# First feed-forward of a two-block transformer: one product in plain float32 from unsplit weights, a new order of the four products, and the first norms reordered

## The chip, the cores and the metric

The kernel runs on one core of one Trainium2 chip. The metric is the device time of one execution in microseconds (us); lower is better. The kernel before took 975.63 us, the median of three runs (975.62, 975.63 and 975.93).

## The reference

The input `x` has 256 positions of 1024 values, and everything is float32. A first block of two layers is followed by a second block. Of the first layer, which is where the change lies, the reference computes:

```python
h = _multiscale_pool(x, pool_w, pool_scale)      # causal window means (2, 4, 8, 16) minus x, times four 256x256 matrices
x = _layernorm(ALPHA * x + h, ln_mix_g[0], ln_mix_b[0])
x = _layernorm(ALPHA * x + _swiglu(x, w_gate[0], w_up[0], w_down[0]), ln_ffn_g[0], ln_ffn_b[0])
```

`_swiglu` is `(silu(x @ w_gate) * (x @ w_up)) @ w_down` with a hidden width of 2816. After that come a differential attention layer with its own feed-forward, and a second block (three token mixers, a gated merge, a feed-forward with a squared relu and a final norm). All of that is untouched by the change.

## The kernel before, in words

**Tiles and products.** The 256 positions are two tiles of 128 rows, `xs[0]` and `xs[1]`. A product is made to float32 accuracy from three fast products: each operand is split into a high part (a rounded copy) and a low part (operand minus high part), and `mm3` (L315 to L317) issues high times high, high times low and low times high, all in the fast `float32r` type. `XTh` and `XTl` hold the two parts of the transposed activations. `x_transposed` makes them: four transposes on TensorE into a bank of PSUM (L393), a copy on ScalarE for the high part (L308), a subtraction on VectorE for the low part (L309).

**The weight stream.** The class `Stream` carries every weight matrix in *units* of 1 MB, each in two *halves* of 512 KB. `load` puts a half into one of `RAW_BUFS` = 5 raw buffers by DMAs on SyncE's queue (L61); `high` rounds it on ScalarE into `wh` (L92); `low` subtracts on VectorE into `wl` (L101), which frees the raw buffer, and then calls `load` again. Four units can be split ahead of their use (`W_BUFS`). `need(u)` forces what is still missing of unit u, `release` gives a unit's room back, and `side.tick()`, called after each group of products, runs the lows that are outstanding and up to two more highs. Each engine works through its instructions in the order in which they are written here, so a place in the source is a place in the engine's queue.

**The start.** The DMAs are written out by hand: `xs[0]`, the pool weights `pw`, `xs[1]`, a band matrix, then `st.load(2)`, the norm's bias `ln_mix_b`, then `st.load()`. In `load` the line `n = f // len(srcs)` gives a new value to the name that holds the bound, so that the call with 2 goes on until the raw buffers are full.

The pool layer is a small pipeline of its own: `pool_diff` (L704) makes the window differences of a tile on TensorE, `from_psum` (L712) copies them out on ScalarE, `add_tail` (L717) adds to tile 1 what windows take from tile 0, and `pool_product` (L722) multiplies by `pw` in plain float32. In the program a plain float32 matmul is one call, and in the trace it is two instructions. `ln` (L400 to L426) then works on one tile: scaling and residual on VectorE (L408, L409), the mean (L411, L412), the squares on ScalarE (L398), the centred value times gain (L419), the variance (L421), a power on GpSimd (L385), and the last line with the bias (L426). `ln` takes two callbacks, `first` after the squares and `then` after the power, in which the caller puts other work.

**The four products.** `swiglu` calls `ffn`. Its first two chunks of 256 hidden columns (`n_a` = 2) are computed row-wise, for each tile and chunk one bank of 128x512 (gate and up side by side). One product of tile and chunk uses two units (k-tiles 0 to 3 and 4 to 7 of the 1024 inputs): `proj_wide` (L330) issues 12 matmuls of 512 columns for each, 24 in all. Chunk 0 uses units 0 and 1 (halves 0 to 3), chunk 1 uses units 2 and 3 (halves 4 to 7). The order is tile 0 chunk 0, tile 0 chunk 1, tile 1 chunk 0, tile 1 chunk 1. In the middle of the second of them `next(pending)` transposes tile 1. After a product comes its nonlinearity (`post_a`, L596 and L597), and the result is transposed (L542) in the middle of what follows. From the third chunk on, `proj_b` works on both tiles at once with 256 columns.

Of the kernel before, what the change touches and what calls it, by code (L numbers as in the profile page):

```python
# [11 lines left out]
F32 = mybir.dt.float32  # L12
# [5 lines left out]
P = 128  # L18
D = 1024
T = 256  # L20
KT = D // P
D_FF = 2816
# [12 lines left out]
RAW_BUFS = 5  # L35
# [7 lines left out]
class Stream:  # L43


    def __init__(self, nc, pool, units, spare, spare_tile):
        self.nc, self.pool, self.units, self.spare, self.spare_tile = nc, pool, units, spare, spare_tile
        self.raw, self.w, self.pending, self.room = {}, {}, [], W_BUFS
        self.limit = 2 * len(units)
        self.n_dma = self.n_high = self.n_low = self.n_used = 0  # L50

    def load(self, n=None):

        n = 2 * len(self.units) if n is None else n
        while self.n_dma < min(n, self.n_low + RAW_BUFS):
            i = self.n_dma
            srcs, (n_k, f) = self.units[i // 2]
            self.raw[i] = self.pool.tile([P, n_k // 2, f], F32, tag="raw", name=f"raw{i}", bufs=RAW_BUFS)
            n = f // len(srcs)
            for j, src in enumerate(srcs):  # L60
                self.nc.sync.dma_start(self.raw[i][:, :, j * n:(j + 1) * n],  # L61
                                       src[:, i % 2 * (n_k // 2):(i % 2 + 1) * (n_k // 2)])
            self.n_dma += 1

    def high(self, force=False):
        i = self.n_high
        u, half = divmod(i, 2)
        if i >= self.n_dma or i >= self.limit and not force or not half and not self.room and u not in self.spare:
            return False
        n_k, f = self.units[u][1]  # L70
        if not half:
            self.w[u] = [], []
            if u in self.spare:
                self.tiles = [[self.spare_tile("bias", (n_k // 2, f)) for _ in range(2)],
                              [self.spare_tile("qk", (n_k // 4, f)) for _ in range(4)]]
# [12 lines left out]
        n = 0  # L88
        parts = []
        for h in hs:  # L90
            raw = self.raw[i][:, n:n + h.shape[1]]
            self.nc.scalar.copy(h, raw)  # L92
            parts.append((l[:, n:n + h.shape[1]], raw, h.bitcast(F32)))
            n += h.shape[1]
        self.pending.append(parts)
        self.n_high += 1
        return True
# [64 lines left out]
def model_kernel(ctx: ExitStack, tc: tile.TileContext, a: dict, out: bass.AP, stop=None):  # L162
# [13 lines left out]
    def bank(tag):  # L176
        return ps.tile([P, 512], F32, tag=tag, name=nm(tag), bufs=BANKS[tag])
# [4 lines left out]
    def small(n):  # L182
        return gen("sm", (n,))
# [25 lines left out]
    def bcast(src, n=D):  # L209
        t_ = gen("bc", (n,))  # L210
        load(t_, bass.AP(src.tensor, src.offset, [[0, P], [1, n]]))
        return t_
# [69 lines left out]
        load(pw[:, 4 * h:4 * h + 4], a["pool_w"][0, 2 * h:2 * h + 2].rearrange("g (k p) d -> p (g k) d", p=P))  # L282
    load(xs[1], x2[P:T])
    load(band[1], a["c_band"][:, :, 144:272])
    st.load(2)
    ln_gb = ln_g, bcast(a["ln_mix_b"][0])
    st.load()
    side = Side(st)

# [24 lines left out]
    def mm3(o, lh, ll, rh, rl, first, last):  # L314
        nc.tensor.matmul(o, lhsT=lh, rhs=rh, start=first, stop=False)  # L315
        nc.tensor.matmul(o, lhsT=lh, rhs=rl, start=False, stop=False)  # L316
        nc.tensor.matmul(o, lhsT=ll, rhs=rh, start=False, stop=last)  # L317
# [9 lines left out]
        if tick:  # L327
            side.tick()

    def proj_wide(o, t, u, h):  # L330

        wh, wl = st.need(u)
        s = slice(t * P, (t + 1) * P)
        for k in range(KT // 2):
            mm3(o, XTh[:, 4 * h + k, s], XTl[:, 4 * h + k, s], wh[k], wl[k], h == 0 and k == 0, h == 1 and k == 3)
        if t:
            st.release(u)
# [59 lines left out]
    def square(x, acc_col, bias=0.0):  # L397
        nc.scalar.activation(gen(shape=(x.shape[-1],)), x, AF.Square, bias=bias, scale=1.0 / 32.0, accum_out=acc_col)  # L398

    def ln(t, acc, g, b, scale=None, first=None, then=None):  # L400

        x = xs[t]
        sums, var, nm, nm32 = small(2), small(2), small(1), small(1)
        for h, c in enumerate(HALF):
            mix = acc[h]
            if scale is not None:
                mix = gen()
                nc.vector.tensor_mul(mix, acc[h], scale[:, c])  # L408
            nc.vector.scalar_tensor_tensor(x[:, c], x[:, c], ALPHA, mix, op0=ALU.mult, op1=ALU.add,  # L409
                                           accum_out=sums[:, h:h + 1])  # L410
        nc.vector.tensor_scalar(nm32, sums[:, 0:1], sums[:, 1:2], -1.0 / (32.0 * D), op0=ALU.add, op1=ALU.mult)  # L411
        nc.vector.tensor_scalar(nm, sums[:, 0:1], sums[:, 1:2], -1.0 / D, op0=ALU.add, op1=ALU.mult)  # L412
        for h, c in enumerate(HALF):
            square(x[:, c], var[:, h:h + 1], nm32)
        if first:
            first()
        y = [gen(), gen()]
        for h, c in enumerate(HALF):
            nc.vector.scalar_tensor_tensor(y[h], x[:, c], nm, g[:, c], op0=ALU.add, op1=ALU.mult)  # L419
        v = small(1)  # L420
        nc.vector.tensor_scalar(v, var[:, 0:1], var[:, 1:2], LN_EPS, op0=ALU.add, op1=ALU.add)  # L421
        rstd = rsqrt(v)
        if then:
            then()
        for h, c in enumerate(HALF):
            nc.vector.scalar_tensor_tensor(x[:, c], y[h], rstd, b[:, c], op0=ALU.mult, op1=ALU.add)  # L426

# [100 lines left out]
        side.tick()  # L528
        return e1

    def ffn(n_mats, nch, n_a, post_a, gate_b, post_b, end, pending, n_next=4, quota=0, n_late=3, aside={}):
        hT = {}
        us = [st.take(n_mats) for _ in range(n_a)]
        per_bank = 2 // n_mats
# [10 lines left out]
                split_from(tb[:, i * 256:(i + 1) * 256].rearrange("p (k c) -> p k c", k=2),  # L545
                           hT[c][0][:, :, s], hT[c][1][:, :, s])

        for t in range(2):
            for c0 in range(0, n_a, per_bank):
                b = bank("mm")  # L550
                mine = [us[c0 + i // n_mats][i % n_mats] for i in range(2)]
                for i, u in enumerate(mine):
                    proj_wide(b, t, u, i)
                    if not i and not t and c0 + per_bank == n_a:
                        next(pending, None)
                        st.limit = 2 * len(units)
                    if i:
                        if todo:
                            transposed(*todo.pop())
                        mid = post_a(b)  # L560
                    side.tick()
                todo.append((mid, range(c0, c0 + per_bank), t))
        acc = None
        late = []
        for c in range(n_a, nch):
# [24 lines left out]
            return acc, late[-1:], late  # L590
        return finish_layer(acc, end, late[-1:], late, n_next, quota)

    def swiglu(n_a, end, pending, n_next, quota, aside):
        def post_a(b):
            s, m = gen(shape=(256,)), gen(shape=(256,))
            nc.scalar.activation(s, b[:, 0:256], AF.Silu)  # L596
            nc.vector.tensor_mul(m, s, b[:, 256:512])  # L597
            return m

        def gate_b(b):  # L600
            s = gen()
            nc.scalar.activation(s, b, AF.Silu)  # L602
            return s

        def post_b(s, b):
            nc.vector.tensor_mul(s, s, b)
            return s

        return ffn(2, D_FF // 256, n_a, post_a, gate_b, post_b, end, pending, n_next, quota, aside=aside)

# [115 lines left out]
    d0 = [from_psum(pool_diff(0, i), 0, i) for i in range(3)]  # L726
    pb = [pool_product(d0, h) for h in range(2)]
    b1 = [pool_diff(1, i) for i in range(3)]
    d1 = [from_psum(b1[0], 1, 0)]
    st.high()  # L730

    def first0():
        d1.extend(from_psum(b1[i], 1, i) for i in (1, 2))
        for i in range(3):
            add_tail(i)
        st.high()

    ln(0, pb, *ln_gb, pscale, first0, st.low)
    pb = [pool_product(d1, 0)]
    for h, c in enumerate(HALF):  # L740
        x_transposed(xs[0][:, c], 0, h)
    pb.append(pool_product(d1, 1))
    st.need(1)
    st.high()

    def first():
        st.low()
        st.high()

    def then():  # L750
        st.low()
        st.high()

    def end_pool():
        for h, c in enumerate(HALF):
            x_transposed(xs[1][:, c], 1, h)
        yield

    ln(1, pb, *ln_gb, pscale, first, then)
    pending = end_pool()  # L760

    def dump():
# [10 lines left out]
    def load_ln(g, b):  # L773
# [1 line left out]

    pending = swiglu(2, lambda t, acc: end_ln(t, acc, gb1[-1]), pending, 3, 2, {
        2: load_small, 3: lambda: load_ln(a["ln_ffn_g"][0], a["ln_ffn_b"][0]), 4: position_bias,
        5: lambda: spread_bias(0), 6: lambda: spread_bias(4), 7: load_rnn})
    if stop == "ffn0":
        return dump()  # L780

# [462 lines left out]
```

## Time and profile before

| what | value |
|---|---|
| median of three runs | 975.63 us |
| the profiled execution | 975.9 us |
| its span, first to last instruction | 974.1 us |
| granted TensorE clock, mean over the span | 0.994 |
| TensorE matmul busy | 98% of the span |
| VectorE, ScalarE busy | 61%, 50% |
| DMA, share of 16 engines, main queue | 57.5% |

The profiled execution took 1.8 us more than its span. In the rows, PE is TensorE's matmuls, PEld its weight loads, DVE VectorE, ACT ScalarE, POOL GpSimd and SP SyncE; a letter q behind an engine marks its sequencer. Matmuls overlap, so the duration of one is longer than the distance from its start to the next one's. A granted clock of 1.00 is 2.4 GHz and 0.50 is 1.2 GHz. L315 is line 315 of the kernel before.

### The profile page before, as it was taken

How to read it: one execution, taken by the hardware profiler on the slowest of the kernel's cores; microseconds unless marked ns; L12 is line 12 of the kernel's file. 1: busy time of each engine (PE TensorE's matmuls, PEld its weight loads, DVE VectorE, ACT ScalarE, POOL GpSimd, SP SyncE). 2: the span in 40 equal slices, each digit the busy share in tenths (PEclk: the TensorE clock that was granted, in tenths of full speed). 3: DMA queues.
4: the chain of work that ended last, by engine and by line, in shares of the span. 5: the costliest groups of instructions: out<-in, count | busy, mean ns of one | idle time of the engine just before them, and what ended most of it. 6: DMA issues, size and time to landing. Idle time of an engine off the chain costs nothing.

```text
span 974.1 us, 16052 instructions
## 1 busy us (share of the span) xinstructions
PE 951.1 (98%) x6443; PEld 860.7 (88%) x6443; DVE 595.2 (61%) x982; ACT 490.2 (50%) x813; POOL 22.4 (2%) x44
## 2 busy tenths in 40 slices
PE   6999999999999999999998999999999999999997
PEld 5789999988998789999996989998999978899896
DVE  5774554466786864544458468958755676555554
ACT  3553543345666653434445456669644555444441
POOL 1000000000012000000001000000000000000000
PEclk9999999999999999999999999999999999999999
DMA  7576666556635466676752855443655656565531
GB/s 261 152 259 207 216 215 219 174 162 207 191 131 173 144 203 195 218 248 206 270 179 85 253 170 172 149 127 118 194 176 184 225 169 219 184 223 194 180 108 43
DMA packets 134075, 180.22 MB, mean 185 GB/s; under 512 B 8399, under 2 KB 114152, under 8 KB 134000
## 3 DMA queue, kind: packets, MB, share of 16 engines
q1 hardware_dynamic: 133152, 178.34, 57.5%
q8 instruction: 50, 0.82, 0.3%
q10 hardware_dynamic: 848, 0.85, 0.3%
q14 instruction: 25, 0.20, 0.1%
HBM read 178.02 MB, written 5.79 MB: 189 GB/s over the span
## 4 chain that ended last, share of the span: by engine, by line
PE 89%; DVE 5%; ACT 2%; DMA 2%; issue 1%; POOL 1%; POOLq 0%; DVEq 0%; ACTq 0%
PE mm L315 21%; PE mm L316 20%; PE mm L317 20%; PE acc L316 8%; PE acc L317 8%; PE acc L315 8%; DVE wl L101 2%; PE acc L829 1%; PE acc L1099 1%; PE tr L851 1%; DMA raw<-in_w_gate_dram 1%; DMA bc<-in_ln_mix_b_dram 1%; PE tr L393 1%; DMA bc<-in_pool_scale_dram 1%; POOL sm L385 0%
## 5 line engine op out<-in xcount | busy, mean ns | idle before, releaser
L101 DVE TENSOR_TENSOR wl<-raw,wh 128x1024 fp32r<-128x1024 f32 (+1 forms) x314 | 355.2, 1174 | 124.4 <-ACT wh L92 124.2
L92 ACT CAST wh<-raw 128x1024 fp32r<-128x1024 f32 (+1 forms) x314 | 303.1, 1011 | 169.9 <-issue 139.8
L315 PE MATMUL mm<-XTh,wh 128*128 128x256 f32 x1320 | 373.4, 283 | 0.0
L316 PE MATMUL mm<-XTl,wh 128*128 128x256 f32 x1320 | 369.3, 280 | 0.0
L317 PE MATMUL mm<-XTh,wl 128*128 128x256 f32 x1320 | 368.6, 279 | 0.0
L315 PEld LDWEIGHTS mm<-XTh,wh 128*128 128x128 f32 x1320 | 249.3, 189 | 5.8 <-issue 4.0
L316 PEld LDWEIGHTS mm<-XTl,wh 128*128 128x128 f32 x1320 | 247.2, 187 | 1.2
L317 PEld LDWEIGHTS mm<-XTh,wl 128*128 128x128 f32 x1320 | 247.2, 187 | 0.0
L315 PE MATMUL acc<-wh,hh 128*128 128x512 f32 x350 | 139.0, 397 | 0.0
L316 PE MATMUL acc<-wl,hh 128*128 128x512 f32 x350 | 138.1, 395 | 0.0
L317 PE MATMUL acc<-wh,hl 128*128 128x512 f32 x350 | 137.8, 394 | 0.0
L317 PEld LDWEIGHTS acc<-wh,hl 128*128 128x128 f32 x350 | 66.0, 189 | 16.0 <-DVE hl L309 0.4
L315 PEld LDWEIGHTS acc<-wh,hh 128*128 128x128 f32 x350 | 65.8, 188 | 13.8 <-ACT hh L308 0.2
L316 PEld LDWEIGHTS acc<-wl,hh 128*128 128x128 f32 x350 | 65.9, 188 | 13.4
L315 PE MATMUL mm<-wh,XTh 128*128 128x512 f32 (+1 forms) x144 | 54.6, 379 | 0.2 <-ACT XTh L308 0.2
L316 PE MATMUL mm<-wl,XTh 128*128 128x512 f32 (+1 forms) x144 | 53.9, 374 | 0.9 <-DVE wl L101 0.9
L317 PE MATMUL mm<-wh,XTl 128*128 128x512 f32 (+1 forms) x144 | 53.4, 371 | 0.3 <-DVE XTl L309 0.3
L309 DVE TENSOR_TENSOR hl<-rn,hh 128x512 fp32r<-128x512 f32 x30 | 20.8, 693 | 49.8 <-ACT hh L308 49.8
L602 ACT ACTIVATE rn<-mm 128x512 f32<-128x512 f32 x18 | 10.8, 601 | 60.6 <-PE mm L317 60.6
L816 ACT COPY qk<-mm 128x512 f32<-128x512 f32 x22 | 12.9, 588 | 45.0 <-PE mm L317 42.3
L385 POOL TENSOR_TENSOR sm<-sm,mhalf 128x1 f32<-128x1 f32 (+1 forms) x22 | 15.2, 690 | 808.6 <-DVE sm L421 421.0
L316 PEld LDWEIGHTS mm<-wl,XTh 128*128 128x128 f32 x144 | 27.2, 189 | 7.2 <-DVE wl L101 2.4
(209 smaller groups left out, 888.9 us busy)
## 6 DMA issues: line engine op xcount, KB each, us to landing
raw<-in_w_down_dram SPq DMA_DIRECT2D x76, 512.0 KB, 4.5
raw<-in_w_up_dram SPq DMA_DIRECT2D x68, 512.0 KB, 4.6
raw<-in_w_in_dram SPq DMA_DIRECT2D x60, 512.0 KB, 4.4
raw<-in_w_gate_dram SPq DMA_DIRECT2D x36, 512.0 KB, 4.4
raw<-in_w_qkv_dram SPq DMA_DIRECT2D x24, 512.0 KB, 3.6
raw<-in_w_o_dram SPq DMA_DIRECT2D x16, 512.0 KB, 3.5
Rd<-R SPq DMA_DIRECT2D x6, 766.0 KB, 6.7
raw<-in_w_gate_dram SPq DMA_DIRECT2D x16, 256.0 KB, 2.8
```

What stands on the lines that cost most here:

```text
L92: self.nc.scalar.copy(h, raw)
L101: self.nc.vector.tensor_sub(l, raw, h)
L309: nc.vector.tensor_sub(l, src, h.bitcast(F32))
L315: nc.tensor.matmul(o, lhsT=lh, rhs=rh, start=first, stop=False)
L316: nc.tensor.matmul(o, lhsT=lh, rhs=rl, start=False, stop=False)
L317: nc.tensor.matmul(o, lhsT=ll, rhs=rh, start=False, stop=last)
L385: nc.gpsimd.tensor_tensor(r2, v, mhalf.to_broadcast([P, n]) if n > 1 else mhalf, ALU.pow)
L393: nc.tensor.transpose(b[:, k * P:(k + 1) * P], src[:, k * P:(k + 1) * P], ident)
L602: nc.scalar.activation(s, b, AF.Silu)
L816: nc.scalar.copy(flat(o), b)
L829: nc.tensor.matmul(bs[c][:, SPAN[t]], lhsT=qT[r, j, t * P:(t + 1) * P], rhs=kT[r, j, 0:P * (t + 1)], start=True, stop=True)
L851: nc.tensor.transpose(tb[:, k * P:(k + 1) * P], src[:, k * P:(k + 1) * P], ident)
```

## The change

Tile 0's product with chunk 1 becomes eight plain float32 matmuls of 512 columns. Their weights are the unsplit raw halves 4 to 7, which get places of their own (`fetch_aside`): two buffers of the tag `bias`, and four pieces of 256 KB in the tag `hl`, loaded right behind `ln_mix_b` and ahead of halves 0 to 3 and 8. Halves 4 to 7 are split from there later, for tile 1. The left operand is tile 0 transposed and copied unsplit (`x0`). The three other products follow in the order tile 0 chunk 0, tile 1 chunk 0, tile 1 chunk 1; tile 1 is now transposed in the middle of the second unit of the first of them. `ln` gets four callbacks, one more behind each of its two L419 instructions. In tile 0's norm all copies of tile 1's differences come first and only the three `add_tail` are inside; both `pool_product` calls of tile 1 stand ahead of tile 0's transposes. The work on halves 0 to 3 and the low parts of tile 0 move into and around tile 1's norm.

```diff
     def load(self, n=None):
         n = 2 * len(self.units) if n is None else n
-        while self.n_dma < min(n, self.n_low + RAW_BUFS):
+        while self.n_dma < n:
             i = self.n_dma
...
+            if i not in self.aside:
+                if sum(j not in self.aside for j in range(self.n_low, i)) == RAW_BUFS:
+                    break
+                self.raw[i] = [self.pool.tile([P, n_k // 2, f], F32, tag="raw", name=f"raw{i}", bufs=RAW_BUFS)]
+                self.fetch(i)
+            self.n_dma += 1
...
     load(band[1], a["c_band"][:, :, 144:272])
-    st.load(2)
     ln_gb = ln_g, bcast(a["ln_mix_b"][0])
+
+    for i in (4, 5):
+        st.fetch_aside(i, [gen("bias", (2, 512))])
+    for i in (6, 7):
+        st.fetch_aside(i, [gen("hl", (1, 512)) for _ in range(2)])
+    w_whole = [w[:, k] for i in range(4, 8) for w in st.aside[i] for k in range(w.shape[1])]
     st.load()
...
         for k in range(KT // 2):
+            if k == 2 and middle:
+                middle()
             mm3(o, XTh[:, 4 * h + k, s], XTl[:, 4 * h + k, s], wh[k], wl[k], h == 0 and k == 0, h == 1 and k == 3)
...
         for h, c in enumerate(HALF):
             square(x[:, c], var[:, h:h + 1], nm32)
-        if first:
-            first()
+        between[0]()
         y = [gen(), gen()]
         for h, c in enumerate(HALF):
             nc.vector.scalar_tensor_tensor(y[h], x[:, c], nm, g[:, c], op0=ALU.add, op1=ALU.mult)
+            between[1 + h]()
...
         rstd = rsqrt(v)
-        if then:
-            then()
+        between[3]()
...
+        order = [(t, c0) for t in range(2) for c0 in range(0, n_a, per_bank)]
+        if whole is not None:
+            order.remove((0, 1))
+            todo.append((post_a(whole), [1], 0))
...
+                proj_wide(b, t, u, i, next_tile if whole is not None and not t and i else None)
...
     b1 = [pool_diff(1, i) for i in range(3)]
-    d1 = [from_psum(b1[0], 1, 0)]
+    d1 = [from_psum(b1[i], 1, i) for i in range(3)]
+    ln(0, pb, *ln_gb, pscale, (lambda: add_tail(0), lambda: (add_tail(1), add_tail(2)), None, None))
+    pb = [pool_product(d1, h) for h in range(2)]
+
+    st.limit = 4
+    x0 = []
+    for h, c in enumerate(HALF):
+        b = bank("tr")
+        for k in range(4):
+            nc.tensor.transpose(b[:, k * P:(k + 1) * P], xs[0][:, 512 * h + k * P:512 * h + (k + 1) * P], ident)
+        x0.append((b.rearrange("p (k c) -> p k c", k=4), slice(4 * h, 4 * h + 4), gen("gt")))
+        nc.scalar.copy(x0[h][2], b)
+    whole = bank("mm")
+    for k in range(KT):
+        nc.tensor.matmul(whole, lhsT=x0[k // 4][2][:, k % 4 * P:(k % 4 + 1) * P], rhs=w_whole[k],
+                         start=k == 0, stop=k == KT - 1)
+    for b, ks, _ in x0:
+        nc.scalar.copy(XTh[:, ks, 0:P], b)
+
+    def x0_low(h):
+        b, ks, _ = x0[h]
+        nc.vector.tensor_sub(XTl[:, ks, 0:P], b, XTh[:, ks, 0:P].bitcast(F32))
+
     st.high()
 
-    def first0():
-        d1.extend(from_psum(b1[i], 1, i) for i in (1, 2))
-        for i in range(3):
-            add_tail(i)
-        st.high()
-
-    ln(0, pb, *ln_gb, pscale, first0, st.low)
-    pb = [pool_product(d1, 0)]
-    for h, c in enumerate(HALF):
-        x_transposed(xs[0][:, c], 0, h)
-    pb.append(pool_product(d1, 1))
-    st.need(1)
-    st.high()
-
-    def first():
+    def after_stats():
+        x0_low(0)
         st.low()
         st.high()
-
-    def then():
+        x0_low(1)
         st.low()
-        st.high()
+
+    ln(1, pb, *ln_gb, pscale, (st.high, None, lambda: (st.low(), st.high()), after_stats))
...
-    ln(1, pb, *ln_gb, pscale, first, then)
     pending = end_pool()
```

## Rows read from the trace of the kernel before

**Rows 1.** The page, busy us (share of the span) xinstructions.

```profile
PE 951.1 (98%) x6443; PEld 860.7 (88%) x6443; DVE 595.2 (61%) x982; ACT 490.2 (50%) x813; POOL 22.4 (2%) x44
```

**Rows 2.** Stages: stretch and length, PE, PEld, DVE, ACT, POOL, granted clock, DMA share, GB/s.

```profile
14.00:17.00 3.00, 2.22 (x13) 1.53 (x11) 1.01 (x7) 3.00 (x8) 0.00 (x0) 1.00 1.11 351
17.00:21.00 4.00, 0.61 (x2) 0.21 (x2) 3.40 (x7) 0.81 (x1) 1.38 (x1) 0.92 0.44 157
...
21.00:22.00 1.00, 0.83 (x4) 0.87 (x5) 0.68 (x2) 0.00 (x0) 0.00 (x0) 0.50 0.82 248
26.00:27.00 1.00, 1.00 (x4) 0.81 (x3) 1.00 (x2) 0.56 (x1) 0.00 (x0) 0.50 0.22 23
...
28.00:30.00 2.00, 2.00 (x11) 1.60 (x10) 1.93 (x5) 0.00 (x0) 0.00 (x0) 1.00 0.86 240
```

**Rows 3.** Waits of PE after 60 us: line, what it waited for, us, times, longest.

```profile
PE mm L317 <- DVE XTl L309: 1.8, 2, 1.5
```

**Rows 4.** Timeline, tile 0's norm: start, us, engine, line, instructions, idle before and its releaser.

```profile
13.83 1.05 ACT L92 CAST wh<-raw 128x1024 fp32r<-128x1024 f32 x1
...
14.78 0.72 ACT L398 ACTIVATE rn<-x,sm 128x512 f32<-128x512 f32 x1
...
16.65 0.21 DVE L717 TENSOR_TENSOR rn<-tr,rn 128x48 f32<-128x48 f32 x1 [1.91 <-ACT rn L712]
...
17.01 1.41 DVE L419 SCALAR_TENSOR_TENSOR rn<-x,sm,bc 128x512 f32<-128x512 f32 x2
18.33 0.21 DVE L421 TENSOR_SCALAR sm<-sm 128x1 f32<-128x1 f32 x1
...
18.70 1.38 POOL L385 TENSOR_TENSOR sm<-sm,mhalf 128x1 f32<-128x1 f32 x1 [16.39 <-DVE sm L421]
...
20.27 1.42 DVE L426 SCALAR_TENSOR_TENSOR x<-rn,sm,bc 128x512 f32<-128x512 f32 x2 [0.60 <-DMA bc<-in_ln_mix_b_dram]
```

**Rows 5.** Timeline of PE, from tile 1's pool products to the first fast products.

```profile
14.80 1.56 PE L722 MATMUL acc<-pw,rn 128*128 128x256 f32 x6 [0.22 <-DVE rn L717]
...
21.16 1.94 PE L393 MATMUL tr<-ident,x 128*128 128x128 f32 x8 [3.55 <-DVE x L426]
22.90 3.62 PE L722 MATMUL acc<-pw,rn 128*128 128x256 f32 x8
25.96 0.99 PE L315 MATMUL mm<-wh,XTh 128*128 128x512 f32 x1
```

**Rows 6.** Timeline of PE, the four products at full clock and their end.

```profile
28.13 0.39 PE L315 MATMUL mm<-wh,XTh 128*128 128x512 f32 x1
28.36 0.40 PE L316 MATMUL mm<-wl,XTh 128*128 128x512 f32 x1
...
34.66 0.50 PE L316 MATMUL mm<-wl,XTh 128*128 128x512 f32 x1 [0.57 <-DVE wl L101]
...
35.95 1.29 PE L393 MATMUL tr<-ident,x 128*128 128x128 f32 x8
...
51.97 0.38 PE L542 MATMUL tr<-ident,rn 128*128 128x128 f32 x2
```

**Rows 7.** Timeline of PE, 11 to 12 us, plain float32 matmuls at full clock.

```profile
10.69 1.67 PE L722 MATMUL acc<-pw,rn 128*128 128x256 f32 x7
```

**Rows 8.** Timeline of SP's queue: raw loads and the norm's bias.

```profile
5.28 0.62 SPq L61 DMA_DIRECT2D raw<-in_w_gate_dram  x1
...
13.81 0.34 SPq L211 DMA_DIRECT2D bc<-in_ln_mix_b_dram  x1
```

**Rows 9.** Tile 1's norm and the split of halves 0 to 3, timeline.

```profile
22.29 0.59 ACT L308 CAST XTh<-tr 128x512 fp32r<-128x512 f32 x1 [4.47 <-PE tr L393]
...
24.37 3.49 DVE L101 TENSOR_TENSOR wl<-raw,wh 128x1024 fp32r<-128x1024 f32 x3
...
27.77 0.68 DVE L408 TENSOR_TENSOR rn<-acc,bc 128x512 f32<-128x512 f32 x1
...
30.56 0.21 DVE L411 TENSOR_SCALAR sm<-sm 128x1 f32<-128x1 f32 x1
```

More of the change, by code (lines that the diff above doesn't have):

```diff
@@ L49, in __init__ @@
         self.limit = 2 * len(units)
+        self.aside = {}
         self.n_dma = self.n_high = self.n_low = self.n_used = 0
@@ L54, in load, with fetch, fetch_aside @@
         n = 2 * len(self.units) if n is None else n
-        while self.n_dma < min(n, self.n_low + RAW_BUFS):
+        while self.n_dma < n:
             i = self.n_dma
-            srcs, (n_k, f) = self.units[i // 2]
-            self.raw[i] = self.pool.tile([P, n_k // 2, f], F32, tag="raw", name=f"raw{i}", bufs=RAW_BUFS)
-            n = f // len(srcs)
-            for j, src in enumerate(srcs):
-                self.nc.sync.dma_start(self.raw[i][:, :, j * n:(j + 1) * n],
-                                       src[:, i % 2 * (n_k // 2):(i % 2 + 1) * (n_k // 2)])
-            self.n_dma += 1
+            u, half = divmod(i, 2)
+            n_k, f = self.units[u][1]
+            if i not in self.aside:
[4 more added lines that the diff above has]
+            self.n_dma += 1
+    def fetch(self, i):
+        u, half = divmod(i, 2)
+        srcs, (n_k, f) = self.units[u]
+        n, k = f // len(srcs), half * (n_k // 2)
+        for dst in self.raw[i]:
+            for j, src in enumerate(srcs):
+                self.nc.sync.dma_start(dst[:, :, j * n:(j + 1) * n], src[:, k:k + dst.shape[1]])
+            k += dst.shape[1]
+    def fetch_aside(self, i, pieces):
+        self.aside[i] = self.raw[i] = pieces
+        self.fetch(i)
     def high(self, force=False):
@@ L89, in high @@
         parts = []
-        for h in hs:
-            raw = self.raw[i][:, n:n + h.shape[1]]
+        pieces = [raw[:, k:k + m] for raw in self.raw[i] for m in [min(raw.shape[1], hs[0].shape[1])]
+                  for k in range(0, raw.shape[1], m)]
+        if len(hs) < len(pieces):
+            hs = [hs[0][:, k:k + 1] for k in range(n_k // 2)]
+        for h, raw in zip(hs, pieces):
             self.nc.scalar.copy(h, raw)
@@ L328, in proj_a, with proj_wide @@
             side.tick()
-    def proj_wide(o, t, u, h):
+    def proj_wide(o, t, u, h, middle=None):
         wh, wl = st.need(u)
@@ L398, in square, with ln @@
         nc.scalar.activation(gen(shape=(x.shape[-1],)), x, AF.Square, bias=bias, scale=1.0 / 32.0, accum_out=acc_col)
-    def ln(t, acc, g, b, scale=None, first=None, then=None):
+    def ln(t, acc, g, b, scale=None, between=(None,) * 4):
         x = xs[t]
         sums, var, nm, nm32 = small(2), small(2), small(1), small(1)
+        between = [w or (lambda: None) for w in between]
         for h, c in enumerate(HALF):
@@ L529, in finish_layer, with ffn @@
         return e1
-    def ffn(n_mats, nch, n_a, post_a, gate_b, post_b, end, pending, n_next=4, quota=0, n_late=3, aside={}):
+    def ffn(n_mats, nch, n_a, post_a, gate_b, post_b, end, pending, n_next=4, quota=0, n_late=3, aside={},
+            whole=None):
         hT = {}
@@ L546, in transposed, with next_tile @@
                            hT[c][0][:, :, s], hT[c][1][:, :, s])
[L548 to L562, printed above, removed]
+        order = [(t, c0) for t in range(2) for c0 in range(0, n_a, per_bank)]
+        if whole is not None:
+            order.remove((0, 1))
+            todo.append((post_a(whole), [1], 0))
+        for t, c0 in order:
+            b = bank("mm")
+            mine = [us[c0 + i // n_mats][i % n_mats] for i in range(2)]
+            last = not t and c0 + per_bank == n_a
+            def next_tile():
+                next(pending, None)
+                st.limit = 2 * len(units)
+            for i, u in enumerate(mine):
+                proj_wide(b, t, u, i, next_tile if whole is not None and not t and i else None)
+                if last and not i and whole is None:
+                    next_tile()
+                if i:
+                    if todo:
+                        transposed(*todo.pop())
+                    mid = post_a(b)
+                side.tick()
+            todo.append((mid, range(c0, c0 + per_bank), t))
         acc = None
@@ L591, in ffn, with swiglu @@
         return finish_layer(acc, end, late[-1:], late, n_next, quota)
-    def swiglu(n_a, end, pending, n_next, quota, aside):
+    def swiglu(n_a, end, pending, n_next, quota, aside, whole=None):
         def post_a(b):
@@ L607, in post_b @@
             return s
-        return ffn(2, D_FF // 256, n_a, post_a, gate_b, post_b, end, pending, n_next, quota, aside=aside)
+        return ffn(2, D_FF // 256, n_a, post_a, gate_b, post_b, end, pending, n_next, quota, aside=aside,
+                   whole=whole)
     R0 = dr.tile([24, NREL], F32, name="R0")
@@ L777, in model_kernel @@
         2: load_small, 3: lambda: load_ln(a["ln_ffn_g"][0], a["ln_ffn_b"][0]), 4: position_bias,
-        5: lambda: spread_bias(0), 6: lambda: spread_bias(4), 7: load_rnn})
+        5: lambda: spread_bias(0), 6: lambda: spread_bias(4), 7: load_rnn}, whole)
     if stop == "ffn0":
```

## The prediction

> **What bounds the kernel now.** The page first: TensorE's matmuls are busy for 98% of the span, VectorE for 61% [rows 1]. A gain must therefore come from TensorE starting its long run earlier, doing less, or running faster. The view by stages shows that all three are open only at the start: PE works for 0.61 us of the 4 us from 17 to 21, and from 21 to 27 us the granted clock is 0.50, that is 1.2 GHz, where it was 1.00 before the pause and is 1.00 again from 28 us [rows 2]. The waits of PE after 60 us are few: the longest in total is 1.8 us, behind low parts of tile transposes, and the stream of weights is not among the large ones [rows 3]. So what the start gains should reach the end.
>
> The timelines show why PE pauses. Tile 1's first pool products start at 14.80 us; then PE waits for tile 0's norm, whose last line (L426) starts at 20.27, and transposes at 21.16 [rows 4, 5]. In that norm the variance (L421) is only computed at 18.33, although its squares began at 14.78: VectorE waited 1.91 us in `add_tail` for copies that stand on ScalarE behind the squares, and only then did the two L419 [rows 4]. After the transposes the second half of tile 1's pool products (22.90 to 25.96) runs at the slow clock ahead of the first fast product [rows 2, 5]. The four products end at 51.97, where the last L542 of that stage begins [rows 6].
>
> I compare two points: the start of L426 (20.27 now) and the end of the four products (51.97).
>
> **Step 1, tile 0's norm.** No arithmetic goes away. The cast of half 0 (13.83, 1.05 us) leaves ScalarE's queue ahead of the squares, and two copies of tile 1's differences enter; the last differences are there by 14.80, when PE goes on [rows 4, 5], so the squares start near 15.0 instead of 14.78 and, at 0.72 us each, are done by about 16.5. VectorE meanwhile does L419 in two parts (1.41 together) with the tails (0.21 each) between, ready at about 16.6. L421 then comes at 16.6 instead of 18.33. From there to L426 it took 1.94 us, 0.37 to the power's start, 1.38 for the power, the rest a wait for the bias [rows 4]. The bias goes out behind the band matrix, at about 5.3 us instead of 13.81 [rows 8], past ten raw loads, so it is no longer last. L426 starts at about 18.4: **1.9 us earlier**. Bounds: 0.9 if one of the reordered pieces meets a buffer still being written by a square, 2.1 if the copies cost nothing.
>
> **Step 2, from L426 to the first matmul of the four products.** Now 20.27 to 25.96, 5.7 us. Afterwards both pool products of tile 1 stand ahead of the transposes: five further matmuls, ten instructions of about 0.215 us (seven in 1.67 us, the last 0.38 long [rows 7]), fill 16.3 to about 18.6. The first L426 half ends at 18.4 + 0.71 = 19.1, so PE pauses for about 0.5 us where it now pauses for 3.55. Eight transposes take 1.29 at full clock [rows 6], stretched to 20.5 by the second half of L426. The new copy of the first bank (0.59 as the cast of that shape [rows 9]) ends at 20.45; the second hides behind the first four k-tiles. First matmul at 20.5: 2.15 us instead of 5.7, **3.5 us less**. Here lies most of the slow clock's price.
>
> **Step 3, the four products.** Now 26.0 us (25.96 to 51.97). At full clock a fast matmul of 512 columns starts 0.23 us after the last [rows 6], so 96 make 22.1; transposes, the slow first matmuls and waits on `wl` as at 34.66 [rows 6] are the rest. Afterwards 24 of the 96 are replaced by eight plain float32 ones. No row has that shape. Lower bound: twice the 256-column price, two instructions of 0.43, 6.9 us for eight. Upper bound at full clock: each instruction as two fast passes of 0.23, 7.4. I take 7.1, as the 256-column row is the nearest kind. So TensorE does **1.6 us more** than in the 5.5 it replaces. The sum: 7.1 + 72 x 0.23 (16.6) + 1.2 for tile 1's transposes + 0.5 for two L542 pairs and the first bank's change = 25.5 us, **0.5 less**.
>
> This needs cover. While the float32 product runs (20.5 to 27.6), ScalarE does `XTh` (two of 0.59), half 0, two squares, halves 1 to 3 (1.05 each), to about 27.7; VectorE does tile 1's norm sums (2.8 us, 27.77 to 30.56 now), two L419, lows of 1.17 (three in 3.49 [rows 9]), two `x0_low`, and tile 1's L426 by 30.6. PE first wants half 1's low part at 29.0 (ready 27.4), `XTl` at 27.9 (ready 26.3), tile 1 in the middle of the second unit at 31.8 (ready 30.6), half 3's low part at 33.0 (ready 32.1). The margins are 0.9 to 1.6 us. The silu of the float32 product and its multiplication stand ahead of half 3's low part, on ScalarE and VectorE; they need the product's end at 27.6 and a table load, and still come before tile 1's L426 is through. `load_small` and later loads keep their places relative to PE. Without cover each of these would cost its lateness in full. For small stalls I allow 0.2 us.
>
> **Step 4, DMAs.** SP now issues 4 + 8 transfers for halves 4 to 7 ahead of ten for halves 0 to 3 and 8. Ten raw loads went out between 5.28 and 13.81, 0.85 us each, paced by the data (351 GB/s, share above 1 [rows 2, 8]). Ahead of and with half 0 there are as many bytes as now altogether, and the busy stretch ends inside 17 to 21 us; half 0 lands by about 20.2, each further half 1.5 us later, half 3 by 24.7. They are wanted on ScalarE at 22.3 and 26.6: 1.9 us to spare, and 1.0 us more in the cover of step 3 for half 0, which makes 23.3 the point from which lateness costs. Half 7 lands near 19, its matmuls run near 26. Halves 4 to 7 free no raw buffer, but half 13 waits for `low(8)` in either kernel, and PE's distance to it stays about 2.5 us (3.2 now).
>
> The trace shows 256 KB transfers, several in flight, moving at 351 GB/s. The Trainium skill (DMA: Bandwidth & Descriptors, Measured) says the opposite of small ones, 138 GB/s at 64 KB and 341 at 1 MB, and asks for batches of 1 MiB. By an estimate from its figure for 64 KB the eight pieces of 128 KB would take 7.6 us instead of 3.0 and put half 0 at 24.8, 1.5 us past that point: by this page the gain would come out 1.5 us smaller. I go by the row.
>
> **The sum.** 1.9 + 3.5 + 0.5 - 0.2 = 5.7 us off the profiled execution's 975.9 gives 970.2; its median is 0.3 lower, so **970.0 us** with rounding. What a measurement of this kernel can tell from no change is about 0.2%, 1.95 us.
>
> **Rivals.** *The clock stays low or falls again.* Now it falls inside the pause ahead of 21.16 (0.92 over the four us from 17 to 21 is 0.64 us at half) and stays at 0.50 until 27, some 6.6 us [rows 2, 5]. If the float32 product met such a stretch, half of it is lost: 3.3 us, **973.3**. Against it: PE would have matmuls from 14.8 to 19.1 almost without a gap. For it: from 19.1 to 20.5 there are only transposes. The Trainium skill (TensorE: Matmul & The Clock Gate, Part 4) says that transposes do not count as matmul activity for the clock; no row here separates that, as transposes stood among matmuls at 1.00 near 36 us. Chance 0.07.
>
> *The gain is given back.* A later wait that does not move with PE, such as the weight stream at the third chunk, would hold the end: **975.6**. Rows 3 show no large one; half 13's margin of 2.5 us speaks for at most a part. Chance 0.06.
>
> *Slower: raw half 0 comes late.* Its cast now stands on ScalarE ahead of tile 1's squares, so everything in step 3's cover queues behind one transfer. Loss begins when it lands after 23.3 and is one for one; past 29.0 the kernel is slower than before, past 31.0 by over 0.2%. Landing at 31.3 it costs 8.0 us and gives **978**. For that the 1.05 MB of small pieces would have to take 14 us instead of 3, 75 GB/s, against 351 in the row. Chance 0.04.
>
> *Smaller gain.* Step 1 at its lower bound, float32 matmuls at 7.4 and stalls of 1 us in the cover: 1.0 + 0.3 + 0.8 less, **972.1**. Chance 0.15. It remains 0.68 for the forecast, whose own range is 969.2 to 971.4: down by 0.2 each for step 1's better bound, the float32 product's lower bound and no stalls, and up to where the smaller gain begins.
>
> **Numbers.** The range 968.8 to 973.2 holds the forecast with 0.3 to spare, the spread of the three runs, the smaller gain and about half of the clock's case. Faster by over 0.2% (below 973.7): 0.68 + 0.15 + 0.05 of the clock's 0.07, 0.88. Within 0.2%: the gain given back, 0.06, and the clock's other 0.02, 0.08. Slower: 0.04.
>
> **What would show it.** Right: L426 of tile 0 near 18.4; no granted 0.50 after 20 us; sixteen float32 instructions of some 0.43 spacing from 20.5 to 27.6; the last L542 of the four products near 46.2; PE's waits after that as now. Wrong: a PE wait on `XTl`, `wl` or `x` between 27 and 35 us (cover gone), ScalarE waiting on a raw DMA before 27 us (step 4), the float32 product over 8 us long, or a wait on `wl` near 57 us when the down projection begins.

## The result, and the profile after

The changed kernel takes 969.22 us (median of 6 runs, 968.45 to 969.95); the kernel before, run beside it, 975.72 (975.62 to 976.24). The ratio is 0.9933, interval 0.992 to 0.9946. The forecast was 970.0, range 968.8 to 973.2. The profiled execution took 969.95 us, its span is 968.2. Lines have moved: L315, L316 and L317 of before are now L339 to L341, L393 is L776 for tile 0, L722 is L759, L398 is L424, L419 is L445, L421 is L448, L385 is L411, L426 is L452, L92 is L111, L101 is L120, L542 is L570; the float32 product is L781.

The view by stages, in the columns of [rows 2]:

```profile
14.00:20.00 6.00, 5.70 (x30) 4.44 (x29) 5.16 (x16) 3.31 (x9) 0.55 (x1) 1.00 0.94 282
20.00:27.00 7.00, 7.00 (x19) 3.27 (x18) 6.89 (x14) 5.49 (x11) 0.66 (x2) 1.00 1.00 331
```

Read the second column and the clock: PE works for 12.7 of these 13 us, and the clock stays at 1.00, where before it fell to 0.50 [rows 2]. The timeline of tile 0's norm, as [rows 4]:

```profile
14.75 0.72 ACT L424 ACTIVATE rn<-x,sm 128x512 f32<-128x512 f32 x1
...
15.60 0.75 DVE L445 SCALAR_TENSOR_TENSOR rn<-x,sm,bc 128x512 f32<-128x512 f32 x1
16.30 0.21 DVE L448 TENSOR_SCALAR sm<-sm 128x1 f32<-128x1 f32 x1
16.67 0.55 POOL L411 TENSOR_TENSOR sm<-sm,mhalf 128x1 f32<-128x1 f32 x1 [14.37 <-DVE sm L448]
17.25 1.41 DVE L452 SCALAR_TENSOR_TENSOR x<-rn,sm,bc 128x512 f32<-128x512 f32 x2 [0.74 <-POOL sm L411]
```

The squares start when they did, the variance comes 2.0 us earlier, and the power takes 0.55 us where it took 1.38. PE's timeline, as [rows 5, 6]:

```profile
14.69 3.72 PE L759 MATMUL acc<-pw,rn 128*128 128x256 f32 x16 [0.22 <-DVE rn L754]
18.25 1.20 PE L776 MATMUL tr<-ident,x 128*128 128x128 f32 x8
19.52 3.70 PE L781 MATMUL mm<-bias,gt 128*128 128x512 f32 x8
23.06 3.60 PE L781 MATMUL mm<-hl,gt 128*128 128x512 f32 x8
26.09 0.80 PE L339 MATMUL mm<-wh,XTh 128*128 128x512 f32 x1
...
44.49 0.38 PE L570 MATMUL tr<-ident,rn 128*128 128x128 f32 x2
```

No row has an idle time in brackets after the first, and the view of PE's waits from 16 to 60 us is empty. The last row, the end of the four products, stood at 51.97: 7.48 us are won here. The last matmuls of the program, after and (second fence) before:

```profile
961.06 0.28 PE L341 MATMUL mm<-wh,hl 128*128 128x256 f32 x1
```

```profile
966.77 0.27 PE L317 MATMUL mm<-wh,hl 128*128 128x256 f32 x1
```

Only 5.71 us are left in this pair; the profiled execution of the changed kernel is the slowest of its six, and by the medians 6.50 us are won. From the end of the four products to the last matmul the changed kernel takes 961.06 - 44.49 = 916.57 us, the kernel before 966.77 - 51.97 = 914.80, for the same matmuls. So **7.48 won, 1.77 lost again**, and the waits do not show the loss: PE's waits after 60 us begin with the same row as [rows 3].

```profile
PE mm L341 <- DVE XTl L333: 1.8, 2, 1.5
```

With the matmuls of both kernels paired one by one from the last backwards, the gain goes down evenly along the execution: 7.45 us for the matmul that started at 60 us in the kernel before, 7.03 at 300 us, 6.42 at 600 us, 5.93 at 900 us. On average the starts of matmuls lie about 0.3 ns further apart (1.77 us over some 6,260). That was in no step of the prediction.

The weights: SP's queue, the casts on ScalarE, the low part of half 3 on VectorE, and the first matmul that reads it:

```profile
13.12 0.33 SPq L74 DMA_DIRECT2D hl<-in_w_up_dram  x1
13.87 0.33 SPq L74 DMA_DIRECT2D hl<-in_w_gate_dram  x1
...
16.51 0.43 SPq L74 DMA_DIRECT2D raw<-in_w_gate_dram  x1
...
20.91 1.07 ACT L111 CAST wh<-raw 128x1024 fp32r<-128x1024 f32 x1
...
26.88 1.06 ACT L111 CAST wh<-raw 128x1024 fp32r<-128x1024 f32 x1 [1.34 <-DMA raw<-in_w_up_dram]
...
30.00 1.22 DVE L120 TENSOR_TENSOR wl<-raw,wh 128x1024 fp32r<-128x1024 f32 x1
...
31.77 0.39 PE L340 MATMUL mm<-wl,XTh 128*128 128x512 f32 x1
```

Half 3 landed at 26.88, not 24.7, and ScalarE waited 1.34 us for it; its low part was still done at 31.22, 0.55 us before PE first read it.

### The profile page after: what moved, and what is told of

Read it like the earlier page. It is cut to its first block, busy times and chain, and to the rows that moved or that the text cites. A ratio compares the mean times of both kernels' runs of the same rounds, so it can differ in the third digit from the quotient of the medians.

```text
span 968.2 us, 16046 instructions
## 1 busy us (share of the span) xinstructions
PE 950.4 (98%) x6435; PEld 857.3 (89%) x6435; DVE 595.2 (61%) x984; ACT 491.2 (51%) x817; POOL 20.6 (2%) x44
## 4 chain that ended last, share of the span: by engine, by line
PE 92%; DVE 4%; ACT 2%; issue 1%; POOL 0%; DMA 0%; POOLq 0%; DVEq 0%; ACTq 0%
PE mm L339 21%; PE mm L341 20%; PE mm L340 20%; PE acc L340 8%; PE acc L341 8%; PE acc L339 8%; PE acc L875 1%; DVE wl L120 1%; PE acc L759 1%; PE mm L781 1%; PE acc L1145 1%; PE tr L897 1%; PE tr L419 1%; ACT rn L424 0%; PE tr L1080 0%
## 5 line engine op out<-in xcount | busy, mean ns | idle before, releaser
L120 DVE TENSOR_TENSOR wl<-raw,wh 128x1024 fp32r<-128x1024 f32 (+1 forms) x310 | 350.3, 1173 | 122.4 <-ACT wh L111 122.2
L111 ACT CAST wh<-raw 128x1024 fp32r<-128x1024 f32 (+1 forms) x310 | 299.1, 1011 | 165.9 <-issue 131.8
L339 PE MATMUL mm<-XTh,wh 128*128 128x256 f32 x1320 | 374.6, 284 | 0.0
L341 PE MATMUL mm<-XTh,wl 128*128 128x256 f32 x1320 | 367.9, 279 | 0.0
L339 PEld LDWEIGHTS mm<-XTh,wh 128*128 128x128 f32 x1320 | 246.6, 187 | 6.0 <-issue 4.0
L341 PEld LDWEIGHTS mm<-XTh,wl 128*128 128x128 f32 x1320 | 248.3, 188 | 0.0
L339 PE MATMUL acc<-wh,hh 128*128 128x512 f32 x350 | 138.4, 396 | 0.0
L341 PE MATMUL acc<-wh,hl 128*128 128x512 f32 x350 | 138.0, 394 | 0.0
L341 PEld LDWEIGHTS acc<-wh,hl 128*128 128x128 f32 x350 | 65.9, 188 | 15.9 <-DVE hl L333 0.4
L339 PEld LDWEIGHTS acc<-wh,hh 128*128 128x128 f32 x350 | 65.6, 187 | 14.7 <-ACT hh L332 0.2
L339 PE MATMUL mm<-wh,XTh 128*128 128x512 f32 (+1 forms) x136 | 51.4, 378 | 0.2 <-ACT XTh L332 0.2
L341 PE MATMUL mm<-wh,XTl 128*128 128x512 f32 (+1 forms) x136 | 50.2, 369 | 0.3 <-DVE XTl L333 0.3
L340 PE MATMUL mm<-wl,XTh 128*128 128x512 f32 (+1 forms) x136 | 50.1, 368 | 0.2 <-DVE wl L120 0.2
L638 ACT ACTIVATE rn<-mm 128x512 f32<-128x512 f32 x18 | 10.8, 599 | 60.8 <-PE mm L341 60.8
L1230 ACT ACTIVATE rn<-mm 128x512 f32<-128x512 f32 x16 | 9.6, 599 | 41.4 <-PE mm L341 41.4
L341 PEld LDWEIGHTS mm<-wh,XTl 128*128 128x128 f32 x136 | 25.5, 188 | 5.7 <-DVE XTl L333 1.2
```

The costliest lines, as they stand in the source:

```text
L120: self.nc.vector.tensor_sub(l, raw, h)
```

## The experiments

Times are medians, where it isn't said that there was one run; the kernel before, run beside each group, took 975.5 to 975.8. "End" is the start of the last L542 or L570 row of the four products.

**The two halves of the change.** First the norms alone: the new order and both pool products ahead, but all four products from split weights.

```diff
-    for i in (4, 5):
-        st.fetch_aside(i, [gen("bias", (2, 512))])
...
-    ln(0, pb, *ln_gb, pscale, (lambda: add_tail(0), lambda: (add_tail(1), add_tail(2)), None, None))
+    ln(0, pb, *ln_gb, pscale, (lambda: add_tail(0), lambda: (add_tail(1), add_tail(2)), None, lambda: (st.high(), st.high())))
...
-    whole = bank("mm")
...
+        x_transposed(xs[0][:, c], 0, h)
+    st.need(1)
     st.high()
```

> Tile 0's norm in the new order and both pool products of tile 1 ahead of the transposes, but all four products from split weights in the old order. Theory A (the float32 product is what gives the splits and tile 1's norm their cover): tile 0's last norm line starts near 17.3 us as in the changed kernel, but PE then waits on low parts of the weights (about 2.4 us near 20 us, about 2 us more near 28 us) and the four products end near 49.6 us instead of 44.5; total near 973.3 us, more if the clock falls in the first of these pauses. Rival B (the float32 product costs 1.4 us more than the 24 fast matmuls and gives nothing): the four products end near 43.1 us and the total is near 967.9.

Measured: 973.96 us, ratio 0.9983 (0.9974 to 0.9993), end 50.01. The waits of PE from 16 to 60 us, and two stages:

```profile
PE mm L335 <- DVE wl L120: 3.1, 4, 2.0
```

```profile
21.00:23.00 2.00, 0.43 (x2) 0.39 (x3) 2.00 (x3) 2.00 (x3) 0.00 (x0) 1.00 0.00 0
...
25.00:27.00 2.00, 2.00 (x6) 1.56 (x5) 1.97 (x3) 0.00 (x0) 0.00 (x0) 0.50 0.86 224
```

Here the early norm only brings PE to a low half that isn't split yet; it waits, works 0.43 of 2 us, and the granted clock is at 0.50 afterwards. The variant puts all low splits behind the transposes; an earlier place for them was not tried. Second, the product alone, with the old norm and the second pool product behind the transposes:

```diff
-    d1 = [from_psum(b1[i], 1, i) for i in range(3)]
-    ln(0, pb, *ln_gb, pscale, (lambda: add_tail(0), lambda: (add_tail(1), add_tail(2)), None, None))
-    pb = [pool_product(d1, h) for h in range(2)]
+    d1 = [from_psum(b1[0], 1, 0)]
+
+    def first0():
+        d1.extend(from_psum(b1[i], 1, i) for i in (1, 2))
...
+    ln(0, pb, *ln_gb, pscale, (first0, None, None, None))
+    pb = [pool_product(d1, 0)]
...
+    pb.append(pool_product(d1, 1))
```

> The float32 product and the new order of products, but tile 0's norm in the old order (copies of tile 1's differences behind the squares) and the second pool product of tile 1 behind tile 0's transposes. Theory A (most of the gain comes from the norm's new order and from filling PE's pause): last norm line near 19.3 us, transposes from 20.05, float32 product from 23.1, the four products end near 48.1 us, total near 972.8; with the clock at half behind the pause up to 3.3 us more, 976. Rival B (the product alone carries the gain): end near 45 us and a total near 970.

Measured: 974.03 us, ratio 0.998 (0.9969 to 0.9991), end 48.43.

```profile
19.36 1.94 PE L782 MATMUL tr<-ident,x 128*128 128x128 f32 x8 [2.56 <-DVE x L452]
```

```profile
19.00:21.00 2.00, 1.64 (x8) 1.67 (x9) 1.97 (x4) 0.51 (x1) 0.00 (x0) 0.54 0.94 277
21.00:23.00 2.00, 2.00 (x8) 1.68 (x7) 0.21 (x2) 1.73 (x5) 0.00 (x0) 0.60 1.02 335
```

The pause is there again, with granted clocks of 0.54 from 19 to 21 us and 0.60 from 21 to 23. One of the eight executions had a mean granted clock of 0.998 over its span, the others 0.995 or 0.996; it took 971.55 us, the others 973.14 to 974.58. That puts the price of the slow clock here at some 2.5 us, by an estimate from these times; no profile of that execution shows it. L452 starts at 18.46 (19.3 expected), 1.8 us earlier than in the kernel before though the norm has its old order: no low split stands beside its power now, the bias comes early, and tile 1's first pool product starts 0.6 us earlier in this execution (14.23 against 14.80).

At the end of the four products the parts are worth 1.96 and 3.54 us, together 7.48: each part removes the wait that the other runs into. These numbers carry the accidents of single executions (the profile of the norms alone is the slowest of its ten). An estimate from the medians, with what each kernel loses behind the four products added back, is 3.0 and 3.3 us against 8.3 for the whole, so about 2 us more than the parts either way. Third, the changed kernel with only the second pool product put back behind the transposes:

```diff
-    pb = [pool_product(d1, h) for h in range(2)]
+    pb = [pool_product(d1, 0)]
...
+    pb.append(pool_product(d1, 1))
```

> The changed kernel with one thing moved back: the second pool product of tile 1 stands behind tile 0's transposes again. PE then pauses about 1.5 us ahead of the transposes. If the clock stays at 1.00 through such a pause: the float32 product starts near 20.95 instead of 19.52 and the four products end 1.4 us later, near 45.9 us; total near 970.6. If a pause of 1.5 us is enough for the clock to fall, up to 3.3 us more: end near 49 us, total near 974.

Measured: 970.87 us, ratio 0.9951 (0.9936 to 0.9966), end 46.03.

```profile
18.29 1.29 PE L776 MATMUL tr<-ident,x 128*128 128x128 f32 x8 [1.47 <-DVE x L452]
```

```profile
19.00:21.00 2.00, 2.00 (x12) 1.82 (x13) 1.11 (x3) 1.92 (x4) 0.00 (x0) 1.00 1.00 317
```

The place of that product is worth 1.5 us, PE's pause alone (1.47), for the clock stayed at 1.00 this time. Fourth, the float32 product computed twice into the same bank:

```diff
-    for k in range(KT):
+    for k in 2 * list(range(KT)):
```

> The changed kernel with the float32 product computed twice into the same bank (the second pass overwrites the first with the same values). If PE is bound there without slack and the product costs what the trace shows, sixteen instructions 0.43 us apart: 6.9 us more, the four products end near 51.4 us, total near 976.1. If part of the product only covers a wait on splits or on tile 1's norm that would be there anyway: less than 6.9 us more.

Measured: 975.84 us, ratio 1.0004 (0.9995 to 1.0013). This execution is 1.6 us earlier than the changed kernel's from tile 1's first pool product on, so the stretch is compared: the product starts at 17.95 and the end is at 49.78, 31.83 later, against 24.97 in the changed kernel: **one product costs 6.86 us**, the lower bound of step 3 (6.62 by the medians).

**Why the power took 0.55 us.** In the kernel before, both powers (1.38 us, and 1.46 in tile 1's norm) ran beside the low split, a VectorE subtraction with both operands in SBUF. One such operation was added beside tile 0's power:

```diff
+    def beside_power():
+        nc.vector.tensor_sub(gen("bc", (4, 256)), pw[:, 0:4], pw[:, 4:8])
+
+    ln(0, pb, *ln_gb, pscale, (lambda: add_tail(0), lambda: (add_tail(1), add_tail(2)), None, beside_power))
```

> The changed kernel with one more VectorE subtraction of 1,024 columns, both operands and the output in SBUF, run beside the rstd power of tile 0's norm. In the kernel before that power took 1.38 us beside such a subtraction, in the changed one 0.55 us with nothing beside it. Theory A (a VectorE operation with both operands in SBUF holds up GpSimd): the power takes about 1.4 us again and ends some 0.4 us after the subtraction; the normalizing operation on L452 starts 0.9 to 1.1 us later than without it, and the gap to the first product's start stays 2.27 us. Rival B (the 0.55 us comes from the new order of the norm, not from what VectorE does): the power stays at 0.55 us, and L452 waits only for VectorE, the subtraction of about 1.1 us instead of the power's 0.55, so 0.5 to 0.6 us later.

```profile
16.37 1.22 DVE L769 TENSOR_TENSOR bc<-pw 128x1024 f32<-128x1024 f32 x1
16.61 1.38 POOL L411 TENSOR_TENSOR sm<-sm,mhalf 128x1 f32<-128x1 f32 x1 [14.30 <-DVE sm L448]
18.03 1.41 DVE L452 SCALAR_TENSOR_TENSOR x<-rn,sm,bc 128x512 f32<-128x512 f32 x2 [0.44 <-POOL sm L411]
```

One run, 970.65 us. The power takes 1.38 us again, and it ends (17.99) 0.40 us behind the subtraction (17.59). From L448 (16.24) to L452 it is 1.79 us against 0.95, so 0.84 more, just under what A said; the gap to the product's start stays (20.23 - 18.03 = 2.20). And with one operand in PSUM:

```diff
+    def beside_power():
+        junk = gen("bc", (2, 512))
+        for h in range(2):
+            nc.vector.tensor_sub(junk[:, h], pb[h], flat(pw[:, 2 * h:2 * h + 2]))
```

> The changed kernel with two more VectorE subtractions of 512 columns each, one operand in PSUM and one in SBUF, run beside the same power. Theory A (only the form with both operands in SBUF holds GpSimd up): the power stays at 0.5 to 0.7 us. Rival C (any VectorE work beside it slows the power): it takes 1.3 us or more, as beside the subtraction with both operands in SBUF.

```profile
16.20 1.28 DVE L771 TENSOR_TENSOR bc<-acc,pw 128x512 f32<-128x512 f32 x2
16.44 0.55 POOL L411 TENSOR_TENSOR sm<-sm,mhalf 128x1 f32<-128x1 f32 x1 [14.13 <-DVE sm L448]
```

One run, 970.06 us. As long a piece of VectorE work leaves the power at 0.55. So B and C fall: what holds GpSimd up is VectorE with both operands in SBUF, for as long as that operation lasts. The Trainium skill (SBUF — State Buffer, SBUF: two separate sides) says this: such an operation and a GpSimd operation that reads SBUF exclude each other for a whole instruction. The trace agrees, with 1.38 against 0.55.

**Where the 1.77 us go.** First both kernels again, unchanged.

> The kernel before, unchanged. Theory A (the 1.8 us of the gain that the profiled pair loses evenly between 50 us and the end belong to the execution, not to the program): counted matmul by matmul against a profile of the changed kernel, the part of the gain that goes after the four products differs by over 0.5 us from the 1.77 of the first pair, and the median stays near 975.6. Rival B (it belongs to where the change puts the program in time): again 1.5 to 2.0 us.

> The changed kernel, unchanged. Both theories: a median within 0.5 us of 969.2. Theory A: the stretch from the end of the four products to the last matmul differs between this profile and the first one of the same kernel by over 0.5 us; rival B: by under 0.3 us.

Measured: 975.73 and 969.18 us. From the 5,900th matmul from the end to the last it is 863.85 and 863.72 us in the two profiles of the kernel before, 865.50 and 865.51 in those of the changed one; the second pair loses 1.91. So it is no accident of an execution: A falls. What the two executions of the changed kernel differ by lies ahead of the first norm (L452 at 17.25 and 16.70).

All variants so far that keep the changed kernel's loads show 865.47 to 865.55, the norms alone 865.03. What these share is where the buffers lie in SBUF. They are placed in the order of their first use; the trace shows no addresses, so the places here are worked out from that order and the sizes in the source. In the kernel before, `st.high()` asks for the first low half ahead of tile 0's norm; now the norm's fourteen small buffers (32 bytes each) come first, and the low halves `wl` begin 448 bytes later within the same stretch. (The buffers of halves 4 to 7 also come earlier and push everything behind them up by 22,528 bytes, eleven times 2,048.) This is tested with not an instruction changed:

```diff
     b1 = [pool_diff(1, i) for i in range(3)]
+    for _ in range(14):
+        small(8)
```

> The kernel before, instruction for instruction; only the fourteen small statistics buffers (448 bytes a partition) are placed ahead of the four buffers of the low weight halves instead of behind them, as the changed kernel's new order of first uses places them, so those four begin 448 bytes higher. Theory A (the loss along the tail comes from where the low halves lie in SBUF): the time from the 5,900th matmul from the end to the last grows from 863.8 us towards the 865.03 of the run with the new norms alone, whose low halves lie at the same address: 864.9 to 865.1, and the median is 976.6 to 977.0. Rival B (it comes from the instructions or from when the stages start): 863.7 to 863.9, and the median stays at 975.6.

Measured: 976.84 us, ratio 1.001 (1.0001 to 1.002). The kernel before loses by this alone: 864.95 us; its four products end at 51.72 and its last matmul, below, starts 916.03 later instead of 914.80.

```profile
967.75 0.28 PE L317 MATMUL mm<-wh,hl 128*128 128x256 f32 x1
```

The reverse, on the changed kernel:

```diff
     b1 = [pool_diff(1, i) for i in range(3)]
+    for i in range(W_BUFS):
+        sb.tile([P, KT // 2, 512], F32R, tag="wl", name=f"wl_first{i}", bufs=W_BUFS)
```

> The changed kernel, instruction for instruction; the four buffers of the low weight halves are placed ahead of the small ones, so they begin 448 bytes lower, at the same place within 2,048 bytes as in the kernel before. Theory A (placement): the last 5,900 matmuls take 863.8 to 864.3 us instead of 865.5, and the median is 967.5 to 968.0, faster than both kernels. Rival B: 865.5 us and 969.2.

Measured: **967.83 us**, ratio 0.9917 (0.9903 to 0.9931), 863.70 us. The four products end as in the changed kernel (44.49), the tail is shorter:

```profile
44.42 0.38 PE L570 MATMUL tr<-ident,rn 128*128 128x128 f32 x2
...
959.08 0.28 PE L341 MATMUL mm<-wh,hl 128*128 128x256 f32 x1
```

959.08 - 44.42 = 914.66 us, that of the kernel before (914.80): the whole loss is back. Theory A holds both ways. Why the same 448 bytes cost 1.10 us in the kernel before (864.95 against 863.85) and 1.80 in the changed one (865.50 against 863.70) stays open. Two further places ask which part of the address counts. With 1,536 bytes of late-used buffers ahead as well:

```diff
     b1 = [pool_diff(1, i) for i in range(3)]
+    wks = [sb.tile([P, P * (t + 1)], F32, name=f"wk{t}") for t in range(2)]
+    for i in range(W_BUFS):
+        sb.tile([P, KT // 2, 512], F32R, tag="wl", name=f"wl_first{i}", bufs=W_BUFS)
...
-    wks = [sb.tile([P, P * (t + 1)], F32, name=f"wk{t}") for t in range(2)]
```

> The changed kernel with two more late-used buffers (1,536 bytes together) placed ahead of the low halves and with the low halves ahead of the small ones, so they begin 1,088 bytes higher than in the changed kernel. Theory A in the form that only this offset counts: the last 5,900 matmuls take another time than 865.5 us, between 863 and 866; in the form that only the kernel's old offset is good: 865.0 or more. Rival B: 865.5 us.

Measured: 967.81 us, one run, 863.76. As 1,536 is three times 512, this shows that the place within 2,048 bytes isn't what counts, and that the old one isn't the only good one. And directly behind `XTl`:

```diff
     XTl = sb.tile([P, KT, T], F32R, name="XTl")
+    for i in range(W_BUFS):
+        sb.tile([P, KT // 2, 512], F32R, tag="wl", name=f"wl_first{i}", bufs=W_BUFS)
```

> The changed kernel, instruction for instruction, with the four buffers of the low weight halves placed directly behind the transposed activations: they begin 25,280 bytes lower than in the changed kernel, which is 448 bytes lower by the remainder modulo 256 and not by the remainder modulo 512. Theory A1 (only a remainder within 256 bytes or less counts): the last 5,900 matmuls take 863.6 to 863.9 us again, and the median is 967.6 to 968.0. Theory A2 (the place within 512 bytes or more counts): another time, from 864 to 866 us, with a median of 968.2 or more.

Measured: 967.27 us, ratio 0.9917 (0.9903 to 0.993), 863.59, on another chip, where the kernel before took 975.50. A1 holds: the good starts agree modulo 256 bytes, not modulo 512, and the bad ones (448 bytes off) differ by 192 modulo 256. What is shown is that these places differ; which remainders are good, why a matmul minds, and whether it is the start of `wl` by itself or its place relative to the other operands, stays open; no other remainder was tried. 967.27 and 967.83 overlap in their runs; both beat both kernels.

## Why the prediction was right, point by point

The number was right partly by luck, because two errors met: the steps won more than their 5.7 us, and a loss that no step had took most of the surplus. Against the forecast, in the profiled pair, step 1 won 1.1 us more, step 2 0.1 less and step 3 with its stalls 0.7 more, which makes 7.48; then 1.77 were lost. What failed is the sentence that what the start gains should reach the end.

- *Step 1* said 1.9 us, with 2.1 as its better bound; it was 20.27 - 17.25 = 3.0, outside its bounds. The order was as told, the variance came at 16.30 (16.6 forecast). Mis-sized was the power, taken over from [rows 4] at 1.38 us. That duration belonged to the low split beside it, which the same change moves away; the runs with an operation beside the power show it, 0.84 us of the missing 1.1. The early bias was a condition for all of this: in the second profile of the kernel before the variance came at 17.56 instead of 18.33, and L426 still started at 20.23, after 1.33 us of waiting for the bias. No run moved the bias alone.
- *Step 2* said 2.15 us from L452 to the first matmul of the four products; 2.27 was measured. PE's pause did not shrink, it vanished: the pool products fill the time up to the transposes.
- *Step 3* said 25.5 us and small stalls of 0.2; it was 24.97 without any. The float32 product went to its lower bound, 6.86 against 7.1. The covers held, but half 3's low part by half a microsecond only: PE's first matmul that reads it starts at 31.77, it was ready at 31.22.
- *Step 4* had the first half right, cast at 20.91 without a wait, and half 3 wrong by 2.2 us (26.88 instead of 24.7). The pieces of 128 KB leave SP's queue 0.75 us apart from 13.12 on, and the row's 351 GB/s did not carry over: 282 from 14 to 20 us, 331 from 20 to 27. ScalarE waiting on a raw load before 27 us was one of the prediction's own signs that this step is wrong, and it came; the margin hid the delay. The Trainium skill (DMA: Bandwidth & Descriptors, Measured) has small transfers slower than large ones, in a table of transfers issued from GpSimd. The trace agrees in the direction, but not in the estimate drawn from it: half 0 was put at 24.8, and its cast started at 20.91. No run changes the size of the pieces alone.
- *The rivals.* The clock did not fall in the changed kernel. The smaller gain and late raw data did not come. "The gain is given back" did come in part, but not by its mechanism: no wait on the weight stream, but 1.77 us by the place of `wl` in SBUF. The prediction treated the tail as the same instructions at the same price; buffers placed by their first use let the new order of the norm change the spacing of matmuls that the change doesn't touch.
- *Its sums.* The terms of step 3 add up to 25.4, not 25.5, and the lower end of the forecast's own range is 969.4 by its three terms, not 969.2; neither matters here.

Without that loss the steps are worth what the moved kernels show: 975.76 to 967.83, 7.9 us, and 975.50 to 967.27, 8.2 us.

## What to carry to other kernels

A duration read beside other work belongs to that neighbourhood: before it goes into a sum, ask whether the change takes the neighbour away. Moving a first use can move a buffer, and here 448 bytes cost 0.13% to 0.21% over the last 5,900 matmuls; when a gain fades evenly with no wait to show for it, compare matmul spacings and hold the addresses fixed. And test halves of a change together as well as apart: here 1.96 and 3.54 us made 7.48, and one profile of each isn't enough to add them up to the tenth.

## What the hardware showed that was not expected

- The same matmuls run 863.6 to 863.9 us or 865.0 to 865.6 for the last 5,900, by the place of one set of operands, at a granted clock of 1.00 in both, and repeat within 0.2 us in two executions of a program.
- A one-column GpSimd power takes 0.55 us, and 1.38 beside a VectorE subtraction of 1,024 columns with both operands in SBUF.
- In the variant with a pause of 2.56 us ahead of 19.36 us the granted clock was 0.54 from 19 to 21 us; in the one with a pause of 1.47 us ahead of 18.29 it was 1.00 there. Transposes and pool products came next in both.
- A plain float32 matmul of 512 columns is issued as two instructions 0.43 us apart, 0.86 us in all (6.86 for eight).
